# Token-pair products near the diagonal: 32 by 32 blocks in place of masked 128 by 128 products, in a two-layer backbone

## The chip, the core and the metric

One core of a Trainium2 chip runs the whole program as one launch. The metric is device time in microseconds (us); the time before is the median of three runs. The engines are TensorE (PE; its weight loads are PEld), VectorE (DVE), ScalarE (ACT), GpSimd (POOL) and SyncE (SP, which issues the weight transfers).

## The reference, cut to what matters

Two layers run over 256 context tokens and 256 latent tokens with 1024 features. In each layer one projection feeds three groups of heads: a differential attention, a latent attention and a gated recurrence that runs in both directions (HGRN2, 4 heads, 128 key features, 64 value features). After that come an output projection and an MLP. The change touches the recurrence alone. Its forward half is, cut down:

```
def step(S, xs):                       # one chunk of tokens
    qc, kc, vc, gc = xs                # gc: logarithm of the forget gate, per token and key feature
    b = jnp.cumsum(gc, axis=-2)
    o_inter = jnp.einsum('bhtk,bhkv->bhtv', qc * jnp.exp(b), S)
    rel = jnp.where(mask, b[..., :, None, :] - b[..., None, :, :], 0.0)
    decay = jnp.where(mask, jnp.exp(rel), 0.0)
    A = jnp.einsum('bhtsk,bhsk->bhts', qc[..., :, None, :] * decay, kc)
    o = o_inter + jnp.einsum('bhts,bhsv->bhtv', A, vc)
    b_last = b[..., -1:, :]
    S_new = jnp.exp(b_last[..., 0, :])[..., None] * S + jnp.einsum('bhsk,bhsv->bhkv', kc * jnp.exp(b_last - b), vc)
    return S_new, o
```

A holds, for each pair of tokens t and s of a chunk, the product of query t and key s with the decay between them. The backward half does the same on the reversed tokens, and the two outputs are added.

## The kernel before, in words

All activations stay on the chip, features on partitions. In phase one of a layer the linear products of the combined projection run on PE (lines 140 to 142 with weights on the stationary side, 218 to 220 with tokens on it); each operand is split into two parts, so each tile takes three products. Weights come in units of 128x1024: a transfer, a cast on ACT (line 135) and a subtraction on DVE (line 136).

Beside the linear products runs the recurrence, as a generator (`hg_gen`) of which one step is taken every 3072 columns of linear products (`along`, `pump`). It works on two heads (g) and on a pair of 128-token chunks (pr), so four 128x128 products stand side by side (two chunks of two heads). `hg_intra(g, pr)` builds A for such a set; it is called with queries six times: four times in layer 0 and twice in layer 1, where only the latent tokens have queries. The decays are taken in by doubling the block size m = 1, 2, 4, ..., 64. At each level m the tokens of neighbouring blocks of m are paired: keys `KE` (copied to `Kt` by ACT, line 700, so that the halves of both directions lie in one tile) times queries `QP` (read in place, with an access pattern that hops between the two directions every m tokens). Then `KE`, `QP` and `Fg` are multiplied by the gates of the neighbouring block (DVE, lines 722, 725 and 727), which the next level needs.

Before the change, the pairs of a token with itself (line 691, operand `kd`) and the levels 1, 2, 4 and 8 (line 704) are full 128x128 products, four per level; the first is copied to the tile `AT` by ACT (line 692), and each later one is put into `AT` where a mask says that the pair belongs to that level (DVE, line 705, 128x512). Level 16 (line 712) is formed in blocks of 32 by 32, four blocks along each diagonal, each in its own quarter of the PE columns (`tile_position=(0, j)`), into the PSUM tile `psb`; levels 32 and 64 (lines 717 and 719) go into the same tile, off the diagonal. A last masked copy takes `psb` into `AT` (line 731). `hg_inter` then multiplies `AT` by the values (line 779).

The order in which each engine takes its instructions is not the order of the code: a scheduler places them. PSUM tiles with the tag `sc` come from two banks; the tag `Kt` in SBUF has two buffers.

Of the kernel before, what the change touches and what calls it, by code (L numbers as in the profile page):

```python
# [8 lines left out]
F32 = mybir.dt.float32  # L9
F32R = mybir.dt.float32r  # L10
I32 = mybir.dt.int32
U8 = mybir.dt.uint8
# [14 lines left out]
def mix(t, m, base, nblk, two):  # L27
    """Walks blocks of 2m elements; the second half of each block sits `two` away from the first."""
    p = t.ap[0]
    return bass.AP(t.tensor, t.offset + base, [[p[0], p[1]], [2 * m, nblk], [two, 2], [1, m]])  # L30


def mixT(t, m, base, nblk, two):
    """One value per half block, repeated over its m elements."""
    p = t.ap[0]
    return bass.AP(t.tensor, t.offset + base, [[p[0], p[1]], [2 * m, nblk], [two, 2], [0, m]])
# [3 lines left out]
def net(ctx: ExitStack, tc, x, c, cx, c_ctx, w_mod, b_mod, g_mix, g_mlp, w_in, w_out, da_lambda, da_subln_g,  # L40
# [13 lines left out]
    # ---------------------------------------------------------------- constants  # L54
# [6 lines left out]
    masks = const.tile([128, 5, 128], U8, name="masks")  # L61
# [10 lines left out]
    # ---------------------------------------------------------------- startup loads  # L72
# [33 lines left out]
    # silu of the conditioning, as zero-padded stationary columns  # L106
# [7 lines left out]
    # ---------------------------------------------------------------- weights  # L114
# [5 lines left out]
    def wunit(W, r0, ks, ranges):  # L120
        """Row tiles ks x the given column ranges of W, split in two f32r parts that add up to it."""
        n = sum(w for _, w in ranges)
        nk = len(ks)
# [20 lines left out]
    def lin_fm(W, r0, ranges, nk, rhs, T, evac, shift=None, mid=None, late=None, order=None, fine=False, units=()):  # L144
        """Feature-major product: out[col, tok] over nk row tiles; rhs(k) gives the two parts. With shift, evac
        comes after all products and gets the two columns of the weights' product with the shift too."""
# [59 lines left out]
    def lin_tm(W, ranges, lhs, tiles, evac, nsel):  # L206
        """Token-major product: out[tok, col]; tiles are token tiles, nsel(t) the columns wanted of them."""
# [17 lines left out]
    # ---------------------------------------------------------------- small helpers  # L225
    def rstd_small(ss, n, dim, tagp="rs"):
        """1/sqrt(ss/dim + eps) on a small tile: a first guess by bits, three Newton steps."""
# [11 lines left out]
    def rows_to_bcast(ps, rstd, n):  # L239
        """ps[:, tok] = rstd of that token on every partition."""  # L240
# [5 lines left out]
    def stats(accs, n):  # L246
        """Sum over partitions of the sum of accs[:, tok] into [tok, tile]."""
# [9 lines left out]
    def sq_update(k, T0):  # L257
        """Adds the squares of row tile k of the residual to the running sum; the last stay apart."""
# [17 lines left out]
    class Norm:  # L276
        """Modulated norm of the residual's columns T0:, as two f32r parts. They first hold the residual with its
        gain alone: products with it can run before the statistics are there, and take rstd and the product
        with the shift afterwards. full() then puts the whole norm in its place."""
# [7 lines left out]
        def shift(self):  # L287
            """The shift as stationary columns: upper parts, lower parts, zeros."""
# [39 lines left out]
        def apply(self, ps, c):  # L328
            """rstd times ps, and the columns of the product with the shift."""
# [25 lines left out]
        def first(self, W, ranges, evac, whole=True):  # L355
            """The first products, on the gained residual; then the whole norm."""
# [21 lines left out]
    # ---------------------------------------------------------------- modulation vectors  # L378
# [35 lines left out]
    def mod_beside(l):  # L414
        """The modulation of layer l summed over rows on the vector engine, 1024 columns at a time."""
# [40 lines left out]
    # tokens, feature-major  # L456
# [14 lines left out]
    # first norm: its shift and scale come in four parts of the features  # L471
# [60 lines left out]
    maskf = st_.tile([128, 5, 128], F32, name="maskf")  # L532
# [3 lines left out]
    # lambda, lower bounds, gains  # L536
# [44 lines left out]
    def fill_end():  # L581
        """Finishes the group under way, so that its PSUM bank is free."""
        if fillers and started:
            while started and fillers:
                fill(1)
# [5 lines left out]
    # ================================================================ one layer  # L591
    def layer(l):
# [26 lines left out]
        def pump(gs, n):  # L619
            """n steps of the first live generator of gs."""  # L620
# [4 lines left out]
        # ---- HGRN2: two heads (g) at a time, tokens in two pairs (pr) of 128-token chunks  # L625
# [50 lines left out]
        def hg_intra(g, pr):  # L676
            """Products of all token pairs inside a chunk, block size doubling; per-token decays to the chunk's ends."""
# [3 lines left out]
            hgs[g, pr] = st = {}  # L681
            if withq:
                qc = hq[g][:, pr - pr0].rearrange("p c h t -> p (c h) t")
                st["QP"] = QP = hp.tile([128, 2, 4, 128], F32, tag="QP", name="QP", bufs=2)
                st["AT"] = AT = hp.tile([128, 4, 128], F32, tag="AT", name="AT", bufs=2)
                kd = hp.tile([128, 4, 128], F32, tag="Kt", name="kd", bufs=2)
                V.tensor_add(out=kd, in0=kc[:, 0], in1=kc[:, 1])
                V.tensor_mul(out=QP, in0=fc, in1=qc.unsqueeze(1).to_broadcast([128, 2, 4, 128]))
                ps = psum("sc", (128, 4, 128))
                for h in range(4):  # L690
                    PE.matmul(ps[:, h, :], kd[:, h, :], qc[:, h, :], start=True, stop=True)
                S.copy(out=AT, in_=ps)
                psb = None
                yield
            for lv, m in enumerate((1, 2, 4, 8, 16, 32, 64)):
                nb = 64 // m
                if withq:
                    if m <= 16:
                        Kt = hp.tile([128, 4, 128], F32, tag="Kt", name="Kt", bufs=2)
                        S.copy(out=Kt.rearrange("p h (b t m) -> p (h b) t m", t=2, m=m), in_=mix(kc, m, 0, 4 * nb, m + D))  # L700
                    if m <= 8:
                        ps = psum("sc", (128, 4, 128))
                        for h in range(4):
                            PE.matmul(ps[:, h, :], Kt[:, h, :], mix(QP[:], m, 128 * h + D, nb, m - D), start=True, stop=True)  # L704
# [732 lines left out]
```

## Time and profile before

| | |
|---|---|
| time, median of three runs | 1263.15 us (1262.95 to 1263.32) |
| span of the profiled execution | 1264.6 us |
| PE busy | 1229.0 us (97%) |
| DVE busy | 893.1 us (71%) |
| ACT busy | 577.7 us (46%) |
| POOL busy | 103.2 us (8%) |

The profiled execution shows its span, from the first to the last instruction, and no other time of its own; it is 1.45 us above the median of the runs. The recurrence with queries lies between 74 and 215 us (layer 0) and between 870 and 965 us (layer 1). In the rows an fp32 matmul appears as two records, so a level of four 128x128 products is "x8" and a level of sixteen 32x32 products is "x32". A matmul's duration runs on beside the next ones; what a group takes of PE is read from its start to the start of the next one's.

### The profile page before, as it was taken

Reading aid. Unit: us, or ns where it says so; the run is one execution under the profiler, and the core shown is the slowest. Engines: PE = TensorE matmul, PEld = TensorE weight load, DVE = VectorE, ACT = ScalarE, POOL = GpSimd, SP = SyncE. Lnnn points to the kernel's source line nnn. Section 1 sums busy time; section 2 is a strip of 40 time slices with the busy share of each in tenths; the row PEclk is TensorE's granted clock in tenths of the full one; section 3 lists DMA queues with packets and bytes.
Section 4 is the critical chain, followed back from the end, with each engine's and each line's share of the span. In section 5 each row is a group of like instructions: output and inputs, shape, how many; then the busy total and the mean of one; then the engine's idle time right before and its main releaser. Section 6 shows DMA issues by size and latency. Waiting matters only on the chain.

```text
span 1264.6 us, 20080 instructions
## 1 busy us (share of the span) xinstructions
PE 1229.0 (97%) x7646; PEld 989.8 (78%) x7646; DVE 893.1 (71%) x1732; ACT 577.7 (46%) x1096; POOL 103.2 (8%) x144
## 2 busy tenths in 40 slices
PE   6999999999999999999999999999999998999997
PEld 4678888855558877778787878778898668999997
DVE  4574577766686698756677674696878876865864
ACT  3433333476674374311243332373335885553653
POOL 2200000212100010000000000050002421000000
PEclk8999999999999999999999999999999999999999
DMA  9521221536553327555555554334223413556652
GB/s 327 168 84 51 72 67 53 150 115 196 177 178 104 116 83 216 181 167 167 158 160 167 167 161 139 84 84 111 78 66 112 123 30 104 181 185 185 189 189 71
DMA packets 138336, 171.14 MB, mean 135 GB/s; under 512 B 10898, under 2 KB 116048, under 8 KB 138240
## 3 DMA queue, kind: packets, MB, share of 16 engines
q1 hardware_dynamic: 134960, 164.39, 43.1%
q0 software_dynamic: 2704, 4.94, 1.6%
q8 instruction: 60, 0.98, 0.3%
q10 hardware_dynamic: 576, 0.53, 0.1%
q14 instruction: 36, 0.29, 0.1%
HBM read 160.52 MB, written 1.05 MB: 128 GB/s over the span
## 4 chain that ended last, share of the span: by engine, by line
PE 87%; DVE 6%; ACT 2%; issue 1%; POOL 1%; DMA 1%; SPq 1%; POOLq 0%; DVEq 0%; ACTq 0%
PE mm L140 21%; PE mm L142 21%; PE mm L141 21%; PE sc L1222 3%; PE tp L889 2%; PE mm L392 2%; PE sc L704 2%; PE sc L1208 2%; PE mm L220 2%; PE mm L218 2%; PE mm L219 2%; PE mm L912 1%; PE sc L779 1%; PE sc L750 1%; DVE wl L136 1%
## 5 line engine op out<-in xcount | busy, mean ns | idle before, releaser
L135 ACT CAST wh<-raw 128x1024 fp32r<-128x1024 f32 (+2 forms) x204 | 210.7, 1035 | 328.4 <-PE mm L141 253.8
L136 DVE TENSOR_TENSOR wl<-raw,wh 128x1024 fp32r<-128x1024 f32 (+2 forms) x201 | 243.4, 1212 | 135.1 <-ACT wh L135 132.6
L140 PE MATMUL mm<-mhh,wh 128*128 128x512 f32 (+1 forms) x512 | 174.6, 341 | 0.8 <-DVE fz L336 0.8
L140 PE MATMUL mm<-fa,wh 128*128 128x512 f32 (+1 forms) x512 | 173.7, 340 | 0.0
L141 PE MATMUL mm<-fb,wh 128*128 128x512 f32 (+1 forms) x512 | 173.3, 339 | 0.0
L141 PE MATMUL mm<-mhl,wh 128*128 128x512 f32 (+1 forms) x512 | 173.2, 338 | 0.0
L142 PE MATMUL mm<-fa,wl 128*128 128x512 f32 (+1 forms) x512 | 173.2, 339 | 0.0
L142 PE MATMUL mm<-mhh,wl 128*128 128x512 f32 (+1 forms) x512 | 172.5, 338 | 0.4 <-DVE wl L136 0.4
L140 PE MATMUL mm<-hh,wh 128*128 128x512 f32 (+1 forms) x336 | 127.0, 383 | 4.5 <-ACT hh L351 3.6
L141 PE MATMUL mm<-hl,wh 128*128 128x512 f32 (+1 forms) x336 | 128.0, 381 | 2.7 <-DVE hl L352 2.7
L426 DVE SCALAR_TENSOR_TENSOR room<-raw,scm,room 128x1024 f32<-128x1024 f32 x84 | 106.3, 1286 | 33.1 <-DMA raw<-in_w_mod_dram 32.9
L142 PE MATMUL mm<-hh,wl 128*128 128x512 f32 (+1 forms) x336 | 127.3, 379 | 0.9 <-DVE wl L136 0.9
L140 PEld LDWEIGHTS mm<-mhh,wh 128*128 128x128 f32 x512 | 96.2, 188 | 15.4 <-ACT wh L135 2.5
L140 PEld LDWEIGHTS mm<-fa,wh 128*128 128x128 f32 x512 | 96.4, 188 | 14.2 <-ACT wh L135 2.5
L142 PEld LDWEIGHTS mm<-mhh,wl 128*128 128x128 f32 x512 | 96.2, 188 | 12.5 <-DVE wl L136 0.8
L142 PEld LDWEIGHTS mm<-fa,wl 128*128 128x128 f32 x512 | 96.4, 188 | 11.7
L141 PEld LDWEIGHTS mm<-fb,wh 128*128 128x128 f32 x512 | 96.5, 189 | 11.6
L141 PEld LDWEIGHTS mm<-mhl,wh 128*128 128x128 f32 x512 | 96.4, 188 | 11.2
L140 PEld LDWEIGHTS mm<-hh,wh 128*128 128x128 f32 x336 | 63.9, 192 | 15.7 <-ACT hh L351 4.5
L141 PEld LDWEIGHTS mm<-hl,wh 128*128 128x128 f32 x336 | 63.9, 190 | 14.5 <-DVE hl L352 4.2
L142 PEld LDWEIGHTS mm<-hh,wl 128*128 128x128 f32 x336 | 64.0, 190 | 12.2 <-DVE wl L136 1.4
L347 POOL TENSOR_TENSOR nt<-nt,bc 128x256 f32<-128x256 f32 x24 | 27.0, 1130 | 498.2 <-ACT bc L326 447.4
(332 smaller groups left out, 2236.6 us busy)
## 6 DMA issues: line engine op xcount, KB each, us to landing
raw<-in_w_ff_dram SPq DMA_DIRECT2D x128, 512.0 KB, 3.7
raw<-in_w_mod_dram SPq DMA_DIRECT2D x80, 512.0 KB, 3.7
raw<-in_w_in_dram SPq DMA_DIRECT2D x42, 512.0 KB, 3.9
mraw<-in_w_mod_dram SPq DMA_DIRECT2D x32, 256.0 KB, 6.0
raw<-in_w_out_dram SPq DMA_DIRECT2D x10, 512.0 KB, 3.8
raw<-in_w_in_dram SPq DMA_DIRECT2D x16, 256.0 KB, 5.0
raw<-in_w_in_dram SPq DMA_DIRECT2D x8, 384.0 KB, 3.4
K<-dah POOLq DMA_DIRECT2D x48, 64.0 KB, 2.1
```

Source lines behind the costliest of these rows:

```text
L135: S.copy(out=wh, in_=raw)
L136: (low.pop() if low else V).tensor_sub(out=wl, in0=raw, in1=wh.bitcast(F32))
L140: PE.matmul(ps, lh, rh, start=start, stop=False)
L141: PE.matmul(ps, lh, rl, start=False, stop=False)
L142: PE.matmul(ps, ll, rh, start=False, stop=stop)
L218: PE.matmul(ps, a, wh[:, k, 0:w], start=st, stop=False)
L219: PE.matmul(ps, a, wl[:, k, 0:w], start=False, stop=False)
L220: PE.matmul(ps, b, wh[:, k, 0:w], start=False, stop=sp)
L347: G.tensor_mul(out=ts, in0=ts, in1=self.bc[:, a - T0:b - T0])
L392: PE.matmul(ps[32 * j:32 * j + 32, :], scm[:, k, :], raw[:, 512 * q:512 * q + 512], start=(k == 0), stop=(k == KT - 1))
L426: V.scalar_tensor_tensor(out=acc[r], in0=raw, scalar=scm[:, k, r:r + 1], in1=acc[r], op0=ALU.mult, op1=ALU.add)
L1222: PE.matmul(op[64 * r:64 * r + 64, 0:128], v[:, j, 64 * c:64 * c + 64], PT[:, js], start=(j == 0), stop=(j == nk - 1), tile_position=(0, 6 ...
```

## The change

The pairs of a token with itself and the levels 1 to 8 are formed like level 16 before: 16 products of 32x32 for four 128x128 blocks along the diagonal, each in its quarter of the PE columns. The products of two levels are issued by one call of the new `blocks` (self and 1; 2 and 4; 8 and 16) and share one PSUM tile of 128x2x4x32. They are gathered in an SBUF tile `NR` of 128x4x32: the first is copied by ACT, the next four are put in by DVE with masks of 32 columns. Level 16 goes into `psb`, with 32 and 64. For m = 2 and 8 the queries are copied to a tile `Qt` first (ACT), because `QP` is multiplied on before the products are issued. At the end ACT copies the whole of `psb` to `AT`, and four DVE copies of 32 partitions put `NR` into the diagonal blocks where the pair lies within 16 tokens. The tag `Kt` gets three buffers, `AT` one buffer in layer 1, and the masks shrink from 128x5x128 to 128x5x32. Comments were taken out too, which the diff here leaves out.

```diff
         def hg_intra(g, pr):
             withq = pr in prs
             fc = Fg[g][:, pr].rearrange("p d c h t -> p d (c h) t")
             kc = KE[g][:, pr].rearrange("p d c h t -> p d (c h) t")
             hgs[g, pr] = st = {}
+            pend = []
+            def blocks(near, far=None):
+                ps = psum("sc", (128, 2, 4, 32))
+                for n, (kk, qq) in enumerate(pend):
+                    for h in range(4):
+                        for j in range(0, 128, 32):
+                            o = ps[j:j + 32, n, h, :] if n == 0 or far is None else far[j:j + 32, h, j:j + 32]
+                            PE.matmul(o, kk[:, h, j:j + 32], qq(h, j), start=True, stop=True, tile_position=(0, j))
+                for n in range(len(near)):
+                    if near[n] is None:
+                        S.copy(out=NR, in_=ps[:, n])
+                    else:
+                        V.copy_predicated(out=NR, mask=masks[:, near[n], :].unsqueeze(1).to_broadcast([128, 4, 32]),
+                                          data=ps[:, n])
+                pend.clear()
             if withq:
                 qc = hq[g][:, pr - pr0].rearrange("p c h t -> p (c h) t")
                 st["QP"] = QP = hp.tile([128, 2, 4, 128], F32, tag="QP", name="QP", bufs=2)
-                st["AT"] = AT = hp.tile([128, 4, 128], F32, tag="AT", name="AT", bufs=2)
-                kd = hp.tile([128, 4, 128], F32, tag="Kt", name="kd", bufs=2)
+                NR = hp.tile([128, 4, 32], F32, tag="NR", name="NR", bufs=1)
+                kd = hp.tile([128, 4, 128], F32, tag="Kt", name="kd", bufs=3)
                 V.tensor_add(out=kd, in0=kc[:, 0], in1=kc[:, 1])
                 V.tensor_mul(out=QP, in0=fc, in1=qc.unsqueeze(1).to_broadcast([128, 2, 4, 128]))
-                ps = psum("sc", (128, 4, 128))
-                for h in range(4):
-                    PE.matmul(ps[:, h, :], kd[:, h, :], qc[:, h, :], start=True, stop=True)
-                S.copy(out=AT, in_=ps)
+                pend.append((kd, lambda h, j: qc[:, h, j:j + 32]))
                 psb = None
                 yield
             for lv, m in enumerate((1, 2, 4, 8, 16, 32, 64)):
                 nb = 64 // m
                 if withq:
                     if m <= 16:
-                        Kt = hp.tile([128, 4, 128], F32, tag="Kt", name="Kt", bufs=2)
+                        Kt = hp.tile([128, 4, 128], F32, tag="Kt", name="Kt", bufs=3)
                         S.copy(out=Kt.rearrange("p h (b t m) -> p (h b) t m", t=2, m=m), in_=mix(kc, m, 0, 4 * nb, m + D))
-                    if m <= 8:
-                        ps = psum("sc", (128, 4, 128))
+                        if m in (2, 8):
+                            Qt = hp.tile([128, 4, 128], F32, tag="Kt", name="Qt", bufs=3)
+                            S.copy(out=Qt.rearrange("p h (b t m) -> p (h b) t m", t=2, m=m),
+                                   in_=mix(QP[:], m, D, 4 * nb, m - D))
+                            pend.append((Kt, lambda h, j, Qt=Qt: Qt[:, h, j:j + 32]))
+                        else:
+                            pend.append((Kt, lambda h, j, m=m: mix(QP[:], m, 128 * h + D + j, 16 // m, m - D)))
+                            if m == 16:
+                                psb = psum("sc", (128, 4, 128))
+                                blocks([3], psb)
+                            else:
+                                blocks([None, 0] if m == 1 else [1, 2])
+                    else:
                         for h in range(4):
-                            PE.matmul(ps[:, h, :], Kt[:, h, :], mix(QP[:], m, 128 * h + D, nb, m - D), start=True, stop=True)
-                        V.copy_predicated(out=AT, mask=masks[:, lv, :].unsqueeze(1).to_broadcast([128, 4, 128]), data=ps)
-                    else:
-                        if m == 16:
-                            psb = psum("sc", (128, 4, 128))
-                        for h in range(4):
-                            if m == 16:
-                                for j in range(0, 128, 32):
-                                    PE.matmul(psb[j:j + 32, h, j:j + 32], Kt[:, h, j:j + 32],
-                                              mix(QP[:], m, 128 * h + D + j, 1, m - D), start=True, stop=True,
-                                              tile_position=(0, j))
-                            else:
-                                for j in range(0, 128, 2 * m):
-                                    PE.matmul(psb[j:j + m, h, j + m:j + 2 * m], kc[:, 0, h, j:j + m],
-                                              QP[:, 0, h, j + m:j + 2 * m], start=True, stop=True, tile_position=(0, j))
-                                    PE.matmul(psb[j + m:j + 2 * m, h, j:j + m], kc[:, 1, h, j + m:j + 2 * m],
-                                              QP[:, 1, h, j:j + m], start=True, stop=True, tile_position=(0, j + m))
+                            for j in range(0, 128, 2 * m):
+                                PE.matmul(psb[j:j + m, h, j + m:j + 2 * m], kc[:, 0, h, j:j + m],
+                                          QP[:, 0, h, j + m:j + 2 * m], start=True, stop=True, tile_position=(0, j))
+                                PE.matmul(psb[j + m:j + 2 * m, h, j:j + m], kc[:, 1, h, j + m:j + 2 * m],
+                                          QP[:, 1, h, j:j + m], start=True, stop=True, tile_position=(0, j + m))
                 km = mix(kc, m, 0, 4 * nb, m + D)
                 V.tensor_mul(out=km, in0=km, in1=mixT(fc, m, m, 4 * nb, D - m))
                 if withq:
@@ -728,11 +742,15 @@
                 if m < 16 or not withq:
                     yield
             if withq:
-                V.copy_predicated(out=AT, mask=masks[:, 4, :].unsqueeze(1).to_broadcast([128, 4, 128]), data=psb)
+                st["AT"] = AT = hp.tile([128, 4, 128], F32, tag="AT", name="AT", bufs=1 if last else 2)
+                S.copy(out=AT, in_=psb)
+                for j in range(0, 128, 32):
+                    V.copy_predicated(out=AT[j:j + 32, :, j:j + 32], data=NR[j:j + 32],
+                                      mask=masks[j:j + 32, 4, :].unsqueeze(1).to_broadcast([32, 4, 32]))
                 yield
```

The other lines of the diff are the mask's shape and values, and `bufs=3` where the tag `Kt` is used:

```diff
-    masks = const.tile([128, 5, 128], U8, name="masks")
+    masks = const.tile([128, 5, 32], U8, name="masks")
...
-    masks = [((s // (2 * m) == t // (2 * m)) & (s // m != t // m)) for m in (1, 2, 4, 8)]
-    masks.append(s // 16 != t // 16)
+    r = np.arange(128)[:, None] % 32
+    t = np.arange(32)[None, :]
+    masks = [((r // (2 * m) == t // (2 * m)) & (r // m != t // m)) for m in (1, 2, 4, 8)]
+    masks.append(r // 16 == t // 16)
```

Where the scheduler places the work, first on PE at the second call with queries (layer 0, first heads, second pair of chunks). L140 to L142 are linear products; in the kernel before, L691 is the product of the tokens with themselves and L704 are levels 1 and 2:

```order
L142 MATMUL mm<-hh,wl 128x512
L691 MATMUL sc<-hq_640,kd 128x128 x4
L704 MATMUL sc<-QP,Kt 128x128 x4
L140 MATMUL mm<-hh,wh 128x512
L141 MATMUL mm<-hl,wh 128x512
L704 MATMUL sc<-QP,Kt 128x128 x4
L142 MATMUL mm<-hh,wl 128x512
```

The same place in the changed kernel, where L691 is the matmul of `blocks` and its operands tell the level (kd: tokens with themselves; QP,Kt: level 1; Qt,Kt: level 2):

```order
L142 MATMUL mm<-hh,wl 128x512
L691 MATMUL sc<-hq_640,kd 32x32 x16
L691 MATMUL sc<-QP,Kt 32x32 x16
L140 MATMUL mm<-hh,wh 128x512
L141 MATMUL mm<-hl,wh 128x512
L140 MATMUL mm<-hh,wh 128x512
L691 MATMUL sc<-Qt,Kt 32x32 x16
L141 MATMUL mm<-hl,wh 128x512
```

Three linear products instead of two stand between level 1 and level 2. Level 4 follows 11 linear products later in both kernels.

On ACT, at the first call in layer 0 (L700 and L715 are the copies to Kt, L135 the casts of weight units):

```order
-L692 COPY AT<-sc 128x512
-L700 COPY Kt<-KE_638 128x512 x2
-L135 CAST wh<-raw 128x1024
-L700 COPY Kt<-KE_638 128x512 x2
-L135 CAST wh<-raw 128x1024
+L694 COPY NR<-sc 128x128
+L718 COPY Qt<-QP 128x512
+L135 CAST wh<-raw 128x1024
+L715 COPY Kt<-KE_638 128x512 x2
+L718 COPY Qt<-QP 128x512
+L715 COPY Kt<-KE_638 128x512
+L135 CAST wh<-raw 128x1024
```

The copy of 512 elements out of PSUM has become one of 128, and the two copies to Qt stand ahead of casts that stood there without them.

## Rows read from the trace of the kernel before

**Rows 1.** Page: busy time of each engine; the chain that ended last, by engine
```profile
PE 1229.0 (97%) x7646; PEld 989.8 (78%) x7646; DVE 893.1 (71%) x1732; ACT 577.7 (46%) x1096; POOL 103.2 (8%) x144
PE 87%; DVE 6%; ACT 2%; issue 1%; POOL 1%; DMA 1%; SPq 1%; POOLq 0%; DVEq 0%; ACTq 0%
```

**Rows 2.** Stretches: busy us (instructions) of PE, PEld, DVE, ACT, POOL; PE clock; DMA
```profile
74.00:215.00 141.00, 138.05 (x1038) 116.99 (x1037) 97.10 (x181) 47.36 (x78) 0.00 (x0) 0.99 0.22 60
...
870.00:965.00 95.00, 94.56 (x731) 84.45 (x730) 74.21 (x171) 34.22 (x58) 1.78 (x4) 1.00 0.25 66
```

**Rows 3.** Groups by line on PE: records, busy us, mean ns, idle before
```profile
L704 PE MATMUL sc<-QP,Kt 128*128 128x128 f32 x192 | 30.0, 302 | 2.4 <-DVE QP L725 1.8 <-DVE rs L236 0.4
...
L712 PE MATMUL sc<-QP,Kt 128*32 128x32 f32 x192 | 2.8, 199 | 0.0
```

**Rows 4.** PE in order of time, first call: start us, duration us, records
```profile
74.87 1.12 PE L691 MATMUL sc<-hq,kd 128*128 128x128 f32 x8
75.75 0.48 PE L218 MATMUL mm<-wh,hh 128*128 128x512 f32 x1
...
77.22 1.49 PE L704 MATMUL sc<-QP,Kt 128*128 128x128 f32 x8
78.41 0.53 PE L218 MATMUL mm<-wh,hh 128*128 128x512 f32 x1
...
80.72 1.20 PE L704 MATMUL sc<-QP,Kt 128*128 128x128 f32 x8 [0.41 <-DVE QP L725]
81.66 0.49 PE L219 MATMUL mm<-wl,hh 128*128 128x512 f32 x1
...
83.58 1.05 PE L704 MATMUL sc<-QP,Kt 128*128 128x128 f32 x8
84.39 0.48 PE L218 MATMUL mm<-wh,hh 128*128 128x512 f32 x1
...
87.31 1.13 PE L704 MATMUL sc<-QP,Kt 128*128 128x128 f32 x8
88.19 0.48 PE L220 MATMUL mm<-wh,hl 128*128 128x512 f32 x1
...
89.43 0.40 PE L219 MATMUL mm<-wl,hh 128*128 128x512 f32 x1
89.67 0.39 PE L220 MATMUL mm<-wh,hl 128*128 128x512 f32 x1
89.99 0.46 PE L712 MATMUL sc<-QP,Kt 128*32 128x32 f32 x32
90.37 0.50 PE L218 MATMUL mm<-wh,hh 128*128 128x512 f32 x1
```

**Rows 5.** Whom PE waited for, 74 to 215 us: total us, times, longest
```profile
PE sc L704 <- DVE QP L725: 1.3, 3, 0.5
PE mm L140 <- ACT wh L135: 0.9, 1, 0.9
PE sc L704 <- DVE rs L236: 0.4, 1, 0.4
```

**Rows 6.** Stretch after the second call's first waits, columns as in rows 2
```profile
118.40:121.80 3.40, 3.40 (x13) 3.01 (x14) 2.92 (x5) 0.73 (x2) 0.00 (x0) 0.50 0.40 104
```

**Rows 7.** DVE in order of time, first call, levels 1 and 2
```profile
78.82 0.73 DVE L705 COPY_PREDICATED AT<-masks,sc 128x512 f32<-128x512 uint8 x1 [0.76 <-PE sc L704]
...
79.45 1.12 DVE L725 TENSOR_TENSOR QP<-QP,Fg 128x512 f32<-128x512 f32 x1
...
80.61 0.69 DVE L727 TENSOR_TENSOR Fg<-Fg 128x512 f32<-128x512 f32 x1
...
81.41 0.69 DVE L722 TENSOR_TENSOR KE<-KE,Fg 128x512 f32<-128x512 f32 x1
```

**Rows 8.** Groups by line: copies to Kt on ACT; a 128x128 PSUM operation on DVE
```profile
L700 ACT COPY Kt<-KE 128x512 f32<-128x512 f32 x30 | 20.6, 685 | 37.1 <-DVE KE L722 24.5 <-PE sc L750 5.0 <-DVE rs_t L235 3.2
...
L760 DVE TENSOR_TENSOR S<-sc,S 128x128 f32<-128x128 f32 x16 | 3.9, 285 | 2.2 <-PE sc L750 2.2
```

More of the change, by code (lines that the diff above doesn't have):

```diff
@@ L531, in net @@
         nc.sync.dma_start(out=tl, in_=src)
-    maskf = st_.tile([128, 5, 128], F32, name="maskf")
+    maskf = st_.tile([128, 5, 32], F32, name="maskf")
     nc.sync.dma_start(out=maskf, in_=k_mask)
@@ L743, in hg_inter @@
                         PE.transpose(tp[:, 2 * c + h, :], KE[g][:, pr, d, c, h, :], ident)
-                kt = hp.tile([128, 4, 128], F32, tag="Kt", name="ktok", bufs=2)
+                kt = hp.tile([128, 4, 128], F32, tag="Kt", name="ktok", bufs=3)
                 sl = slice(2 * cs[0], 2 * cs[-1] + 2)
@@ L785, in hg_gate @@
             o = obuf[:, 2 * (pr - pr0):2 * (pr - pr0) + 2, :].rearrange("p c (h e) -> p (c h) e", h=4)
-            sq = hp.tile([128, 8, 64], F32, tag="Kt", name="osq", bufs=2)
+            sq = hp.tile([128, 8, 64], F32, tag="Kt", name="osq", bufs=3)
             ss = hp.tile([128, 8], F32, tag="oss", name="oss", bufs=2)
@@ L1394, in constants @@
                 R[i1, i2] = 1.0
-    s = np.arange(128)[:, None]
-    t = np.arange(128)[None, :]
-    masks = [((s // (2 * m) == t // (2 * m)) & (s // m != t // m)) for m in (1, 2, 4, 8)]
-    masks.append(s // 16 != t // 16)
+    r = np.arange(128)[:, None] % 32
+    t = np.arange(32)[None, :]
+    masks = [((r // (2 * m) == t // (2 * m)) & (r // m != t // m)) for m in (1, 2, 4, 8)]
+    masks.append(r // 16 == t // 16)
     return {
```

## The prediction, made before the changed kernel ran

> **What bounds the kernel now.** First the page: PE is busy 97% of the span and makes up 87% of the chain of waits [rows 1]. Then the two stretches in which the recurrence runs beside the linear products: PE is busy 138.05 of 141 us and 94.56 of 95 us at full clock, DVE 69% and 78%, ACT about a third [rows 2]. So in these stretches a microsecond less on PE is a microsecond less in the end, as long as nothing new is waited for. Next the groups by line say how much of it the change touches: L704 is 30.0 us of PE in 192 records, while L712, which makes one level of the same size out of 32x32 tiles, is 2.8 us in as many records for a quarter as many levels [rows 3]. "Busy" counts the tail that runs on beside the next product, so I take the cost from the order of time: from a group's start to the start of the next linear product [rows 4].
>
> **Taken from PE.** In the first call the five groups that go cost 75.75-74.87 = 0.88 us (tokens with themselves), 78.41-77.22 = 1.19 (level 1), 81.66-80.72 = 0.94 (2), 84.39-83.58 = 0.81 (4) and 88.19-87.31 = 0.88 (8), together 4.70 us. Level 16, already in tiles, takes 90.37-89.99 = 0.38 us, and it starts 0.32 us after the product ahead of it where two linear products are 0.24 apart: 0.08 for coming in, 0.46 in all [rows 4]. A call costs 5.16 us without its waits, six calls 31.0 us.
>
> **Put on PE.** Six groups a call with the tile shape of L712, so 36 groups by 0.46 = 16.6 us. The order puts two groups side by side in five places (four times kd and level 1, once levels 8 and 16), which saves 5 times 0.08: 16.2 us. "Two levels issued together" holds for these only; elsewhere the scheduler has put 1 to 11 linear products between the two. Gain on PE: 31.0-16.2 = 14.8 us.
>
> **Level 1's access.** Level 1 reads the queries with a hop at every element; its 1.19 us against 0.81 of level 4 must be that, since the group waited for nothing [rows 4]. In tiles no row shows it. Lower bound: nothing, if the slower reads hide behind the tiles' issue. Upper bound: it still takes 1.19 us as a group, 0.81 more than 0.38, 4.9 us for six calls. I take the tile row stretched in the same ratio, 0.38 x (1.19/0.81 - 1) = 0.18 a call, 1.1 us, because the row nearest in shape is L712, whose four streams run side by side.
>
> The Trainium skill (TensorEngine Tiling (Array Packing), Instruction Overhead) gives every matmul about 60 cycles, however small. At 2.4 GHz that is 25 ns, an estimate from that page; if each record paid it, a level would take 0.80 us and the gain would be gone; the 32 records of L712 take 0.38 us, 12 ns each [rows 4], so the trace has it at most once per product of two records.
>
> **Waits that go.** L704 was idle 2.4 us over all its groups [rows 3], and L140 waited 0.9 us for the cast in the second call [rows 5]. Right behind these the clock stood at 0.50 (1.2 instead of 2.4 GHz) for 3.40 us [rows 6], which cost half of it, 1.7 us. Together 5.0 us.
>
> **Waits that come.** Until now level 2 followed level 1 through the masked copy and the multiplication of QP. Now: 0.41 us from the end of the group's issue to DVE (78.41 to 78.82), 1.12 for L725 [rows 7], then a copy to Qt on ACT like those to Kt, 0.62 to 0.69 [rows 8], and 0.1 for each handover: 2.35 us. Between the two groups the order has 11, 3, 12, 8, 12 and 12 linear products in the six calls, at 0.23 each. That leaves 1.65 us uncovered in the second call and 0.5 in the fourth; in the first, NR's copy and masked copy stand ahead of L725 on DVE's and ACT's path (about 0.5 more), 0.3. Sum 2.4. Before level 4 the chain is L727, L722 (0.69 each, rows 7), a Kt copy and handovers, 2.3 us from the end of L725, against Qt's 0.8, a tile group of 0.46 and 6, 11, 2, 7, 6 and 4 linear products: 0.6 uncovered. Before level 16, with 3, 4, 7, 5, 5 and 0 products, 0.7, nearly all in the sixth call. At the end of a call one masked copy of 0.73 becomes an ACT copy and four small DVE copies (285 ns for 128x128 in rows 8, four of 32 partitions at that price, 1.1): 1 us later, which the 64-wide group, transposes and linear products mostly cover: 0.5. Sum 4.2, and I leave the half clock in the second call, 1.7: 5.9 us against 5.0, a loss of 0.9. Bounds: only the second call's wait stays (1.7), or the waits are twice as long (8.4 + 1.7).
>
> **What lies beside.** DVE loses five masked copies of 0.73 a call and gets eight at about 0.285: 1.4 us less a call. ACT gets two Qt copies and a small NR copy instead of nothing, about 1.7 us a call; at a third busy it hides them except where the chains above name them, and behind them stand the casts for the weights, each a unit ahead of its use. If that cover went, each late cast would cost PE what L140 paid, 0.9 [rows 5]. The smaller masks are loaded at the start, where nothing waits for them: nothing. SP's and POOL's work keeps its place in phase one.
>
> **Sum.** 14.8 - 1.1 - 0.9 = 12.8 us. The profiled execution's span of 1264.6 becomes 1251.8; it is 1.45 above the median of the runs, 1263.15, which becomes 1250.4.
>
> **Rivals.** (1) DVE paces the recurrence, and PE's gain turns into waits: then no more comes than DVE gets back, 6 x 1.4 = 8.4 us, about 1255. For it: the chain of L725, L727 and L722 is in no way shorter. Against: DVE is 69% and 78% busy [rows 2], and L704's waits are 2.4 us in 24 groups. The Trainium skill (same page, PSUM Bottleneck) warns of just that, the copy out of PSUM becoming the limit once the products are faster; here the change shrinks those copies from 512 to 128 elements too, and no run shows DVE as the limit.
> (2) The waits vanish and the half clock with them, level 1 costs nothing extra: 14.8 + 5.0 - 1.7 = 18.1, 1245. For it: the order now has 11 or 12 linear products in four calls where 7 to 12 stood between levels 1 and 2. Against: the second call has three.
> (3) Tiles don't gain where their operands hop or come from new tiles: each group costs what the whole-array group did, no change, 1263. Against: L712 reads the same QP with a hop.
> (4) Slower: at the six places with four or fewer linear products for cover (levels 1 to 2 in the second call, before 4 in the third and sixth, before 16 in the first, second and sixth) PE waits 1.3 us, as long as 0.9 + 0.4 in the second call [rows 5], and the clock falls for 3.40 us as it did there [rows 6]: 3.0 each, 18.0 instead of the 4.7 that I have for these places. That takes 13.3; with level 1 at its upper bound (3.8 more) the kernel comes to 1263.15 - 12.8 + 17.1 = 1267. It decides from a wait of about 1.3 us on; the waits of 0.5 in rows 5 brought no lower clock.
>
> **Chances.** Forecast 0.72, (1) 0.08, (2) 0.08, (3) 0.04, (4) 0.08. With all unknown costs at their ends the forecast reaches from 1245.0 to 1263.15 - 14.8 + 4.9 + 5.1 = 1258.4; (1) and (2) lie in it, so the range is 1245 to 1259, with 0.12 to 0.2 left out. Within 0.2% (2.5 us, what a measurement here can't tell from no change) I put (3) and the near side of (4): 0.05. Slower: 0.07. Faster: 0.88.
>
> **What would show it.** Right: in the first call each 16-product group takes 0.38 to 0.5 us to the next linear product, level 1's at most 0.6; PE's busy time falls by about as much as the span; both stretches of rows 2 shorten, the first by about 9 us, the second by 4. Wrong: groups of 0.8 us and more; waits of PE for Qt or Kt on ACT above 6 us in sum; clock rows at 0.50 in more than one call; or a later stretch that has become longer.

## The result, and the profile after

| kernel | median of runs, us | lowest to highest | ratio to before, 95% interval | span profiled, us |
|---|---|---|---|---|
| before | 1263.24 (4 runs) | 1262.95 to 1265.68 | | 1264.6 |
| changed | 1248.17 (4 runs) | 1246.11 to 1249.50 | 0.9878 [0.9863, 0.9893] | 1247.7 |

The change makes the kernel 15.1 us faster at the medians; the interval allows 13.5 to 17.3. The forecast of 1250.4 was 2.2 us too high, and the gain of 12.8 us 2.3 too small.

The page of the changed kernel, busy time by engine and the chain that ended last, against [rows 1]:

```profile
PE 1213.5 (97%) x8366; PEld 970.1 (78%) x8366; DVE 882.8 (71%) x1750; ACT 586.1 (47%) x1114; POOL 103.4 (8%) x144
PE 88%; DVE 7%; ACT 2%; issue 1%; POOL 1%; DMA 1%; SPq 0%; POOLq 0%; ACTq 0%
```

PE has 720 records more and 15.5 us less busy time; the profiled span is 16.9 us shorter. DVE gives back 10.3 us, which was not what was waited for: PE still makes up 88% of the chain.

The two stretches of the recurrence, columns as in [rows 2]:

```profile
73.00:203.00 130.00, 127.77 (x1526) 103.06 (x1524) 92.57 (x202) 54.61 (x92) 0.00 (x0) 1.00 0.24 65
860.00:955.00 95.00, 94.53 (x986) 81.25 (x986) 79.15 (x200) 40.99 (x74) 5.96 (x12) 1.00 0.30 80
```

PE stays busy nearly throughout and the clock is 1.00 in both; the 3.40 us at 0.50 of [rows 6] have no counterpart between 73 and 203 us. In this profile a stretch at 0.50 stands just behind, at 211 us (shown under "Changed, again").

Groups by line, columns as in [rows 3] (L691 is now the one line of all levels up to 16; L694, L696, L746 and L748 collect the results; L718 copies the queries):

```profile
L691 PE MATMUL sc<-QP,Kt 128*32 128x32 f32 x576 | 8.9, 203 | 0.2
L691 PE MATMUL sc<-Qt,Kt 128*32 128x32 f32 x384 | 5.5, 199 | 0.7 <-ACT Qt L718 0.6
L691 PE MATMUL sc<-hq,kd 128*32 128x32 f32 x192 | 2.8, 199 | 0.0
...
L718 ACT COPY Qt<-QP 128x512 f32<-128x512 f32 x12 | 7.9, 656 | 4.7 <-DVE QP L739 4.2 <-DVE rs_t L234 0.4
L694 ACT COPY NR<-sc 128x128 f32<-128x128 f32 x6 | 1.6, 262 | 7.6 <-PE sc L691 7.6
L746 ACT COPY AT<-sc 128x512 f32<-128x512 f32 x6 | 3.5, 588 | 15.2 <-PE sc L733 15.2
L696 DVE COPY_PREDICATED NR<-masks,sc 128x128 f32<-128x128 uint8 x24 | 7.2, 301 | 0.2 <-PE sc L691 0.2
L748 DVE COPY_PREDICATED AT<-masks,NR 32x128 f32<-32x128 uint8 x24 | 7.1, 295 | 0.4
```

All 36 groups together are 17.2 us of PE in 1152 records; L704 alone was 30.0 in 192 [rows 3]. A masked copy now takes 301 ns, in place of the 0.73 us of [rows 7].

PE in order of time in the first call, as [rows 4] (start us, duration us, records):

```profile
72.89 0.39 PE L220 MATMUL mm<-wh,hl 128*128 128x512 f32 x1
73.21 0.46 PE L691 MATMUL sc<-hq,kd 128*32 128x32 f32 x32
73.60 0.50 PE L218 MATMUL mm<-wh,hh 128*128 128x512 f32 x1
74.03 0.54 PE L691 MATMUL sc<-QP,Kt 128*32 128x32 f32 x32
74.50 0.50 PE L219 MATMUL mm<-wl,hh 128*128 128x512 f32 x1
...
79.20 0.46 PE L691 MATMUL sc<-QP,Kt 128*32 128x32 f32 x32
79.59 0.50 PE L218 MATMUL mm<-wh,hh 128*128 128x512 f32 x1
```

From a group's start to the next linear product the tokens with themselves take 73.60-73.21 = 0.39 us, level 1 with its hop 74.50-74.03 = 0.47, level 4 0.39. In [rows 4] the first two were 0.88 and 1.19.

Whom PE waited for from 73 to 203 us, against [rows 5]:

```profile
PE mm L140 <- ACT wh L135: 1.3, 1, 1.3
PE sc L691 <- ACT Qt L718: 0.6, 1, 0.6
```

**Where the time went.** Both kernels issue the same linear products, so the same one can be found in both, and the time between two of them compared. The 600 from the 120th on, which hold the first four calls, take 222.1 us before and 212.4 after: 9.7 less. The 600 from the 2600th on, which hold the last two, take 152.2 and 146.7: 5.5 less. The start up to the 120th is 3.1 shorter (its clock in part, below), between the two stretches nothing changes, and from the end of the second to the end of the span it is 1.5 longer. Together that makes the 16.9 of the span, within 0.1.

Counted group by group (from the start of the linear product ahead to the start of the one behind, less the 0.233 us that two such are apart), tokens with themselves up to level 16 in all six calls cost 35.85 us before and 19.2 after: 16.65 less.

**The clock between runs.** The same kernel's runs differ by up to 6 us (1245.48 to 1251.41 for the changed one), and each lists its mean granted clock. Over the 64 runs of this study, one span for each kernel and one common slope fit to 0.85 us: 0.69 us longer for every 0.001 of clock. At the same clock the changed kernel's span is 15.8 us shorter than before (95%: 15.1 to 16.4). The table of experiments uses this reading beside the ratios, because it would also take out a loss of clock that a kernel brings about itself.

### The profile page after: what moved, and what is told of

The parts are those of the page before. It is cut to its first block, busy times and chain, and to the rows that moved or that the text cites. A ratio compares the mean times of both kernels' runs of the same rounds, so it can differ in the third digit from the quotient of the medians.

```text
span 1247.7 us, 21546 instructions
## 1 busy us (share of the span) xinstructions
PE 1213.5 (97%) x8366; PEld 970.1 (78%) x8366; DVE 882.8 (71%) x1750; ACT 586.1 (47%) x1114; POOL 103.4 (8%) x144
## 4 chain that ended last, share of the span: by engine, by line
PE 88%; DVE 7%; ACT 2%; issue 1%; POOL 1%; DMA 1%; SPq 0%; POOLq 0%; ACTq 0%
PE mm L140 21%; PE mm L142 21%; PE mm L141 21%; PE sc L1240 3%; PE tp L907 2%; PE mm L392 2%; PE sc L1226 2%; PE mm L218 2%; PE mm L219 2%; PE mm L220 2%; PE sc L797 1%; PE mm L930 1%; DVE wl L136 1%; PE sc L768 1%; PE sc L691 1%
## 5 line engine op out<-in xcount | busy, mean ns | idle before, releaser
L135 ACT CAST wh<-raw 128x1024 fp32r<-128x1024 f32 (+2 forms) x204 | 210.8, 1034 | 311.7 <-PE mm L141 241.5
L140 PE MATMUL mm<-mhh,wh 128*128 128x512 f32 (+1 forms) x512 | 175.1, 342 | 0.8 <-DVE fz L336 0.8
L140 PE MATMUL mm<-fa,wh 128*128 128x512 f32 (+1 forms) x512 | 173.6, 340 | 0.0
L142 PE MATMUL mm<-mhh,wl 128*128 128x512 f32 (+1 forms) x512 | 173.1, 339 | 0.4 <-DVE wl L136 0.4
L142 PE MATMUL mm<-fa,wl 128*128 128x512 f32 (+1 forms) x512 | 173.1, 338 | 0.0
L140 PE MATMUL mm<-hh,wh 128*128 128x512 f32 (+1 forms) x336 | 127.2, 384 | 4.7 <-ACT hh L351 3.4
L142 PE MATMUL mm<-hh,wl 128*128 128x512 f32 (+1 forms) x336 | 126.7, 377 | 0.9 <-DVE wl L136 0.9
L140 PEld LDWEIGHTS mm<-mhh,wh 128*128 128x128 f32 x512 | 96.4, 188 | 15.4 <-ACT wh L135 2.5
L140 PEld LDWEIGHTS mm<-fa,wh 128*128 128x128 f32 x512 | 96.3, 188 | 14.2 <-ACT wh L135 2.5
L142 PEld LDWEIGHTS mm<-mhh,wl 128*128 128x128 f32 x512 | 96.1, 188 | 12.5 <-DVE wl L136 0.8
L142 PEld LDWEIGHTS mm<-fa,wl 128*128 128x128 f32 x512 | 96.4, 188 | 11.7
L141 PEld LDWEIGHTS mm<-mhl,wh 128*128 128x128 f32 x512 | 96.5, 188 | 11.2
L140 PEld LDWEIGHTS mm<-hh,wh 128*128 128x128 f32 x336 | 63.4, 190 | 15.9 <-ACT hh L351 4.2
L141 PEld LDWEIGHTS mm<-hl,wh 128*128 128x128 f32 x336 | 64.2, 191 | 13.7 <-DVE hl L352 4.0
L142 PEld LDWEIGHTS mm<-hh,wl 128*128 128x128 f32 x336 | 64.1, 191 | 12.7 <-DVE wl L136 1.5
```

The source lines that it names most:

```text
L135: S.copy(out=wh, in_=raw)
L140: PE.matmul(ps, lh, rh, start=start, stop=False)
L141: PE.matmul(ps, lh, rl, start=False, stop=False)
L142: PE.matmul(ps, ll, rh, start=False, stop=stop)
```

## The experiments

My theory: PE paces these stretches, a 16-product group costs it 0.46 us in place of 0.8 to 1.2, and the rest is small. Rivals: the gain comes from DVE's smaller copies, from pairing two levels, or from the smaller masks at the start.

| kernel | median, us (runs) | ratio to before, 95% | span at the same clock, against before | against changed |
|---|---|---|---|---|
| tiles alone | 1252.04 (4) | 0.9905 [0.9888, 0.9922] | -12.4 ± 0.9 | +3.3 ± 1.0 |
| products twice | 1261.39 (11) | 0.9977 [0.9968, 0.9985] | -2.6 ± 0.6 | +13.2 ± 0.8 |
| levels one by one | 1249.60 (4) | 0.9890 [0.9872, 0.9909] | -14.7 ± 0.9 | +1.1 ± 1.0 |
| large masks | 1248.81 (4) | 0.9887 [0.9873, 0.9901] | -15.3 ± 0.9 | |
| first copy on DVE | 1250.29 (4) | 0.9892 [0.9874, 0.9909] | -15.4 ± 0.9 | |
| and one last copy | 1248.19 (4) | 0.9885 [0.9870, 0.9900] | -15.9 ± 0.9 | |
| changed, again | 1248.14 (5) | 0.9885 [0.9867, 0.9904] | -15.8 ± 0.7 (with the first 4) | |

**Tiles alone.** The kernel before, with its products in 32x32 tiles and nothing else: masked copies still write 128x512, each level is used at its own step, no copy of the queries.

```diff
-                        ps = psum("sc", (128, 4, 128))
+                        ps = psum("sc", (128, 4, 32))
                         for h in range(4):
-                            PE.matmul(ps[:, h, :], Kt[:, h, :], mix(QP[:], m, 128 * h + D, nb, m - D), start=True, stop=True)
-                        V.copy_predicated(out=AT, mask=masks[:, lv, :]..., data=ps)
+                            for j in range(0, 128, 32):
+                                PE.matmul(ps[j:j + 32, h, :], Kt[:, h, j:j + 32],
+                                          mix(QP[:], m, 128 * h + D + j, 16 // m, m - D), start=True, stop=True,
+                                          tile_position=(0, j))
+                        V.copy_predicated(out=AT4, mask=masks[:, lv, :]..., data=ps.unsqueeze(2).to_broadcast([128, 4, 4, 32]))
```

> The kernel before with one change: the self products and levels 1 to 8 are formed in 32x32 tiles, each level by itself; the masks of 128 columns and the copies of 512 elements per partition (ACT once, DVE 0.73 us each) stay as they were. Products theory (the gain is the time that the groups take on PE): the groups fall from 35.8 us, waits included, to about 17 plus the waits, and since the masked copy is still ahead of L725 these stay at 3 to 6 us or grow by 1 to 2 (the second call has levels 1 and 2 side by side): 1250 to 1254 us, 9 to 13 below before. Copies theory (the gain comes from the shorter masked copies): 1260 to 1263.

Measured: 1252.04 us, 12.4 of the 15.8 us at the same clock. Its groups by line, and PE's waits over the whole span:

```profile
L708 PE MATMUL sc<-QP,Kt 128*32 128x32 f32 x768 | 11.6, 202 | 2.6 <-DVE QP L732 1.9 <-DVE rs_t L234 0.5
...
L711 DVE COPY_PREDICATED AT<-masks,sc 128x512 f32<-128x512 uint8 x24 | 17.7, 737 | 2.0 <-PE sc L708 1.9
```

The masked copies cost DVE 737 ns each, as before, and most of the gain is there all the same: it is PE's. In the second call the wait for the cast is replaced by one of 1.33 us for QP, since the old chain through the masked copy stays. Of the remaining 3.3 us, 2.4 show in the 600 products of the last two calls: 149.1 us here, 146.7 in the changed kernel, though the groups themselves differ by only 0.7 there (5.96 and 5.26).

**Products twice.** The changed kernel, each group's 16 products issued a second time into the same place.

```diff
                             PE.matmul(o, kk[:, h, j:j + 32], qq(h, j), start=True, stop=True, tile_position=(0, j))
+                    for h in range(4):
+                        for j in range(0, 128, 32):
+                            o = ps[j:j + 32, n, h, :] if n == 0 or far is None else far[j:j + 32, h, j:j + 32]
+                            PE.matmul(o, kk[:, h, j:j + 32], qq(h, j), start=True, stop=True, tile_position=(0, j))
```

> The changed kernel with each 16-product group issued twice into the same place, 36 groups more on PE and nothing else. Products theory: each further group costs the 0.39 us that it takes side by side with another, 14.0 us together, so 1260 to 1264 us, about the time before. Rival (the recurrence's chain on DVE and ACT sets the pace and PE has slack beside it): less than half of it, below 1255.

Measured: 13.2 us more than the changed kernel. PE in its first call:

```profile
72.82 0.46 PE L691 MATMUL sc<-hq,kd 128*32 128x32 f32 x32
73.09 0.49 PE L695 MATMUL sc<-hq,kd 128*32 128x32 f32 x32
73.52 0.54 PE L691 MATMUL sc<-QP,Kt 128*32 128x32 f32 x32
73.88 0.53 PE L695 MATMUL sc<-QP,Kt 128*32 128x32 f32 x32
74.34 0.50 PE L218 MATMUL mm<-wh,hh 128*128 128x512 f32 x1
```

The groups cost 14.5 us more in sum, 0.40 each, and 13.2 ± 0.8 of it reaches the end. No operation of DVE or ACT was added, so this is the most direct evidence that PE's time here counts nearly one to one.

**Levels one by one.** The changed kernel without Qt and without the pairs from level 2 on: each of these levels is formed at its own step and, up to level 8, masked into NR in its small shape. The tokens with themselves and level 1 still go together.

```diff
-                        if m in (2, 8):
-                            Qt = hp.tile([128, 4, 128], F32, tag="Kt", name="Qt", bufs=3)
...
-                                blocks([None, 0] if m == 1 else [1, 2])
+                            blocks([None, 0] if m == 1 else [lv])
```

> The changed kernel without pairing from level 2 on: each level's products are issued with their own level, queries read in place with the hop, no copies to Qt; self and level 1 still share one PSUM tile. Tiles, NR and the small masks stay. Products theory: same PE time, the chain from level 1 to level 2 shorter by the Qt copy (0.66 us) but longer by a masked copy (0.30), more PSUM tiles: within 2 us of the changed kernel, 1246 to 1250. Pairing theory (issuing two levels together is worth something): 1251 to 1254, since a wait like those of 0.5 us of L704 before comes back at most of the six calls.

Measured: 1249.60 us, 1.1 ± 1.0 more than the changed kernel at the same clock, and 2.2 ± 1.2 less than tiles alone. So the later pairs bring about 1 us, and what else the changed kernel has beyond the tiles about 2: the small masked copies, and with them the first pair, the third buffer of Kt and the new end of a call, which no run takes apart. In the medians alone neither can be told from nothing. The second call, PE:

```profile
112.54 0.46 PE L691 MATMUL sc<-QP,Kt 128*32 128x32 f32 x32 [1.31 <-DVE NR L696]
```

Pairing moves a wait rather than removing one: 1.31 us here, 1.30 in the changed kernel, both in the second call.

**Large masks.** The changed kernel with masks loaded at 128x5x128 as before, of which 32 columns are used.

```diff
-    masks = const.tile([128, 5, 32], U8, name="masks")
+    masks = const.tile([128, 5, 128], U8, name="masks")
...
-    maskf = st_.tile([128, 5, 32], F32, name="maskf")
+    maskf = st_.tile([128, 5, 128], F32, name="maskf")
```

> The changed kernel with the masks loaded and cast at their old size, 128x5x128, of which only 32 columns are used. The profile of the changed kernel reached the recurrence about 2 us earlier than the one before. Products theory: that was the clock at the start, where the two profiled executions differ, and this kernel takes the time of the changed one within 1 us. Masks theory: the smaller transfer (0.25 MB less) and cast are worth about 2 us, so 2 us slower than the changed kernel.

Measured: 1248.81 us, like the changed kernel (-15.3 ± 0.9 against -15.8 ± 0.7). The first 32 us of before, changed and large masks, in that order (columns as in [rows 2], PE clock third from the end):

```profile
0.00:32.00 32.00, 21.36 (x180) 13.02 (x180) 13.95 (x45) 11.69 (x21) 7.52 (x17) 0.84 1.00 327
```

```profile
0.00:32.00 32.00, 21.52 (x191) 13.96 (x191) 15.61 (x53) 12.55 (x24) 7.79 (x18) 0.95 1.01 326
```

```profile
0.00:32.00 32.00, 21.15 (x186) 13.72 (x187) 14.81 (x51) 11.64 (x21) 7.52 (x17) 0.95 1.01 327
```

The runs exclude the 2 us of the masks theory: large masks cost 0.5 ± 1.0 at the same clock. They don't exclude a smaller price: the DMA share is 1.00 here at 326 GB/s, and the 0.25 MB that the large masks have more would take about 0.75 us of that, an estimate from these rows. The 120th linear product starts at 68.1 us before, 65.0 in the changed kernel and 66.4 with large masks. Of the 3.1 us between the first two, 1.6 are there with large masks too, at the same clock of 0.95 against 0.84. What the other 1.5 are isn't shown: the first linear product starts anywhere from 21.2 to 22.8 us in the profiles of this study, and not later with large masks as a rule.

**First copy on DVE; and one last copy.** In the second call of the changed kernel PE waits 1.30 us for a cast on ACT. PE and ACT there:

```profile
108.01 0.46 PE L691 MATMUL sc<-hq,kd 128*32 128x32 f32 x32
108.28 0.56 PE L691 MATMUL sc<-QP,Kt 128*32 128x32 f32 x32
110.14 0.50 PE L140 MATMUL mm<-hh,wh 128*128 128x512 f32 x1 [1.30 <-ACT wh L135]
...
111.04 0.46 PE L691 MATMUL sc<-Qt,Kt 128*32 128x32 f32 x32
```

```profile
108.88 0.27 ACT L694 COPY NR<-sc 128x128 f32<-128x128 f32 x1 [1.72 <-PE sc L691]
109.04 1.05 ACT L135 CAST wh<-raw 128x1024 fp32r<-128x1024 f32 x1
110.04 0.69 ACT L718 COPY Qt<-QP 128x512 f32<-128x512 f32 x1
```

ACT sat 1.72 us waiting for the products, for a copy of 0.27, with the cast queued behind it. The fifth run puts that copy on DVE; the sixth also replaces the four last masked copies of 32 partitions by one of 128x512.

```diff
-                        S.copy(out=NR, in_=ps[:, n])
+                        V.tensor_copy(out=NR, in_=ps[:, n])
```

```diff
-                for j in range(0, 128, 32):
-                    V.copy_predicated(out=AT[j:j + 32, :, j:j + 32], data=NR[j:j + 32], mask=...)
+                V.copy_predicated(out=AT.rearrange("p h (r t) -> p h r t", r=4),
+                                  mask=near16.rearrange("p (r t) -> p r t", r=4)..., data=NR.unsqueeze(2)...)
```

> The changed kernel with the first copy of each call from PSUM to NR on DVE instead of ACT. In the changed kernel's profile PE waits 1.30 us for a cast of ACT in the second call, and ACT stands behind the NR copy, which waits for PE. Theory (the NR copy holds the cast up): the wait falls to 0.3 to 0.9 us, and the kernel is 0 to 1.5 us faster than the changed one. Rival (the cast is late for another reason, or DVE's chain gets longer by 0.29 us a call and PE waits for that): the wait stays within 0.2 us of 1.3, and the time the same or up to 2 us longer.

> As the run before, and at the end of a call one masked copy of 128x512 (NR repeated over the four column blocks, a mask of 128 columns) instead of four copies of 32 partitions. By the rows that is 0.73 us of DVE instead of four times 0.295, 0.45 less a call, 2.7 us of DVE in all. Theory (PE is the bound and the end of a call is covered): within 1 us of the run before. Rival (the multiplication with the values waits for AT): up to 2 us faster.

Measured: 1250.29 and 1248.19 us, neither better than the changed kernel (1248.17); at the same clock the first is 0.4 ± 1.0 slower, so the theory of a gain is not borne out. With the copy on DVE the cast's wait goes, and this comes, PE and then the clock (columns as in [rows 2]):

```profile
110.98 0.40 PE L140 MATMUL mm<-hh,wh 128*128 128x512 f32 x1
112.69 0.46 PE L691 MATMUL sc<-Qt,Kt 128*32 128x32 f32 x32 [1.31 <-ACT Qt L718]
```

```profile
113.90:117.30 3.40, 3.40 (x9) 2.63 (x10) 3.40 (x5) 1.57 (x2) 0.00 (x0) 0.51 0.63 161
```

The wait is as long as before, one step later in the chain that the forecast had named (level 1, the product of QP, its copy, level 2), and a half-clock window follows it in this profile. The sixth kernel has the wait of 1.3 for Qt too. Its one last copy takes 736 ns in place of four of 295 (1.18 us), and PE was not waiting for those.

**Changed, again.** The changed kernel once more beside these two, as it was.

> The changed kernel once more, nothing edited, to have its time and another profile beside the two runs of this set: 1247 to 1250 us. Clock theory: the groups of the recurrence cost the same 19.2 us on PE within 0.3, and what differs from the first profile is where the clock stands at 0.50 at the start and around 211 us.

Measured: 1248.14 us, so the gain repeats. In its profile the groups cost 19.2 us again, the clock of the first 32 us is 1.00, and there is no half-clock window from 73 to 215 us; in the first profile of the same kernel there is one. Both, the second profile ahead (columns as in [rows 2]):

```profile
203.00:215.00 12.00, 11.57 (x63) 9.32 (x62) 9.78 (x49) 6.29 (x11) 0.62 (x1) 1.00 0.57 144
```

```profile
210.50:215.50 5.00, 5.00 (x17) 3.97 (x17) 3.88 (x27) 0.82 (x2) 0.00 (x0) 0.66 0.65 190
```

That window costs the first profile about 1.5 us: the 25 linear products from the 575th, which lie across it, take 10.1 us there and 8.6 in the second profile, and the 600 from the 120th take 212.4 and 210.9.

## Why the prediction was right, point by point

**What bounds the kernel: right.** PE at 127.77 of 130 us, groups 16.65 us cheaper, 15.1 us at the end; and 14.5 us of products put back cost 13.2.

**Taken from PE, 31.0 us: right.** The groups' 35.85 us before are these 31.0 and 4.85 of waits and half clock, against 5.0 in the forecast's "waits that go". (The 4.85 are the difference, so they hold all that PE lost in the groups' places beyond the stall-free price.) The two agree more closely than their terms do: of the 1.7 us of half clock only 0.65 lies in the groups, the other 1.0 on the linear products behind the second call's level 2, four of which are 0.42 to 0.58 us apart.

**Put on PE, 16.2 us and 1.1 for level 1's access: right in the first, too much in the second.** 19.2 us less the waits of 2.4 are 16.8, where the forecast had 17.3. Level 1 takes 0.47 us against 0.39 of a group whose queries lie in a row: 0.08 a call, 0.5 in six. The step stretched the tile row in the ratio 1.19 to 0.81 of whole-array products; in tiles the hop costs 0.21 of the group, not 0.47. The trace of the changed kernel also bears on the Trainium skill's sentence on the fixed price of a matmul (TensorEngine Tiling (Array Packing), Instruction Overhead): 0.39 us for 16 products, 24 ns each, agrees with about 60 cycles for each product, 25 ns at 2.4 GHz by that page as an estimate, and not for each of its two records. That the price doesn't depend on the number of columns isn't shown, since every product here has 32.

**Waits that come, 4.2 us and 1.7 of half clock: the term that was mis-sized.** In the groups there are 2.4 us: 1.30 in the second call, 0.6 in the fourth (forecast 0.5), the rest too small to name. The place was right and its releaser not: the forecast had level 2 waiting 1.65 us for Qt, and what came last was the cast behind NR's copy on ACT; Qt, right behind it on ACT, was ready at 110.73 us, before its group began at 111.04. The forecast had the late cast as a cost "if that cover went"; it went in one call. The 0.5 at the end of a call is not there: in the trace no engine waits for the four copies into AT (L748), and the groups of levels 32 and 64 cost 7.0 us over all six calls, 7.07 before. The half clock did not follow the second call's wait in the changed kernel's profiles, and did in that of the first copy on DVE, after a wait as long. So the forecast's condition, a wait of about 1.3 us, was met without the fall that it expected; what decides is open.

**Not in the forecast: what happens beside the groups.** The two stretches of linear products shorten by 15.2 us in the first profile, 1.4 less than the groups' 16.65. The half clock at 211 us, which only this profile has, is as much: without it, in the second profile, they shorten by 11.2 and 5.5, 16.7 in all. Smaller things nearly cancel there. The 1.0 us of half clock behind the second call's level 2 is gone, and so is a wait of 0.4 us at the start of the second layer's phase two. But behind the recurrence other pieces of PE's work now stand later against what they wait for: PE's waits for dg (L244) rise from 1.6 to 2.3 us over the span, and the start of the attentions in the second layer takes 0.7 us more between the same two linear products.

**The sum.** 12.8, and 0.5 for level 1, 1.3 and 0.5 for the waits, 1.7 for the half clock that the forecast left in the second call: 16.8, beside 16.65 in the groups. Less the 1.4 us that the first profile falls short of its groups it is 15.4, beside 15.1 at the medians and 15.8 ± 0.7 at the same clock. That the whole time agrees to 0.3 us is partly luck, since the start and the end of the span differ by more than that from profile to profile.

**The rivals.** (1) DVE as the pace: no. It would have held the gain to 8.4 us, and tiles alone, with DVE's copies as long as before, gains 12.4. The Trainium skill's warning of the copy out of PSUM (TensorEngine Tiling (Array Packing), PSUM Bottleneck) did not come true here: no run shows that copy as the limit. (2) No waits and no half clock, 1245: half right. The half clock left the second call (one as long stands at 211 us in the first profile, none in the second), and 2.4 us of waits stayed; the time lies between it and the forecast. (3) No change: no, 0.39 to 0.47 us per group. (4) Slower: no. Of its six places one waited 1.3 us; level 1 came nowhere near its upper bound.

**What it named as signs.** Groups of 0.38 to 0.5 us: yes, 0.39, and level 1 0.47. Busy time falling by about as much as the span: 15.5 and 16.9. Stretches shorter by about 9 and 4 us: 9.7 and 5.5. One sign of being wrong shows too, a later stretch that has become longer: from the end of the second stretch to the end of the span it is 278.7 us before, 280.2 and 280.5 in the two profiles of the changed kernel. Near 1040 us the clock stands at 0.50 for 6.8 us in both, where the kernel before has 3.4 us at 1057; and 300 linear products from the 3500th take 36.3 us in place of 35.3, at a granted clock of 1.00. With large masks, where the clock near 1040 us is the same, the stretch takes 278.6 us, and the 300 products take 35.3 in every experiment but the changed kernel run again. So what makes the 1.5 us, and whether the change does, is open.

**Open.** Why pairing and small copies together are worth 3.3 us in the runs, when the groups show 0.6 of it: 1.0 us is a wait of PE at the start of phase two that tiles alone has and the changed kernel has not; the rest was not followed. Why the 300 products just named differ is open too.

## What to carry to other kernels

Where one engine is busy for 97% of a stretch, price a change by the order of time on that engine, from an operation's start to the next one's, and not by busy durations: the forecast's 0.46 us for a tile group, read from one such row, was 0.47 in 36 groups. Waits that a change may bring are worth naming one by one, but a wait taken away is often replaced by the next in the same chain, as with the copy moved to DVE; only the cover between the two ends of the chain helps. Where runs of one kernel differ by more than the effect in question, compare them at the same granted clock.

## What the runs showed of the hardware

- The clock before the recurrence differs between profiles of nearly the same work: windows at 0.50 (1.2 GHz in place of 2.4) add up to 10.2 us before, 3.4 and 0 in the two profiles of the changed kernel, 13.7 with levels one by one. What it costs is less than half of that, since PE is not busy throughout there (21.4 of the first 32 us before): the 120th linear product starts at 68.1, 65.0, 63.9 and 67.3 us, in that order.
- A 32x32 tile product of 128 rows and 32 columns in f32 costs 24 ns in a group of 16, the same whether its group is issued once (0.39 us) or twice (0.40 more); queries that hop at every element (level 1) add 0.08 us to a group.
- COPY_PREDICATED takes 737 ns at 128x512 and 301 at 128x128 from PSUM, and 295 at 32x128 from SBUF: with a quarter of the partitions it is hardly shorter, though the source differs too.
